# Score products of an attention group claimed early and joined into one run, on one core

## The chip, the cores and the metric

The kernel runs on one core of one Trainium2 chip. The metric is device time in microseconds (us) from the start to the end of one execution; lower is better. The matrix products run on TensorE, which the profile shows as PE (products) and PEld (loads of the stationary operand). VectorE is DVE, ScalarE is ACT, GpSimd is POOL and SyncE is SP. The banks in which products arrive (PSUM) are tiles of 128 rows of 512 float32 values in this kernel.

## The reference

The reference is a network of six layers over 256 positions of width 1024. Layers 0 to 3 each have a mixer, a norm and a feed-forward part; layers 0 and 3 mix by sliding-window attention, layer 1 by three dilated windows, layer 2 by attention within a block. Two further layers follow that have, among other branches, a differential attention. What the change touches is one thing in all of them, the scores of queries against keys:

```python
s = jnp.einsum('bnqhgd,bnkhd->bnhgqk', qb, kb) * (dh ** -0.5)     # layers 0 to 3, dh = 64
s = jnp.where(ok[None, :, None, None], s, NEG)
m = s.max(-1)
p = jnp.exp(s - m[..., None])
...
scores = jnp.einsum('bqhmd,bkhmd->bhmqk', qb, kh)                 # the two layers behind, 64 wide
p = jax.nn.softmax(jnp.where(mask, scores, -jnp.inf), axis=-1)
```

## The kernel before

The 256 positions are two blocks of 128 rows (t = 0 and 1). Each block is a stream of work of its own, written as a Python generator; `run` takes turns between the two and between small tasks that the streams spawn. That sets the order in which the program is written. A scheduler of the language then makes the final order on each engine: of what is ready by its own estimate of times, it takes what was written first (a priority can be raised for a stretch of code), and it hands out buffers. Each engine works its list strictly in that order.

Weights come by DMA as float32 (`raw`) and are split into a high and a low part by ScalarE (line 396) and VectorE (line 400). A projection is then three products per piece, lines 409 to 411, each 128 rows deep and 512 columns wide. These make up most of TensorE's time.

Attention works on groups of four heads. Queries and keys are transposed, so that the 64 values of a head lie on partitions: two heads (`par` = 0 and 1) share a tile, on partitions 0 to 63 and 64 to 127. `scores` (line 614) makes the group's products: for two tiles (`a`), t + 1 blocks of keys (`j`) and the two halves (`par`), so 4 products for t = 0 and 8 for t = 1. Each uses 64 rows of the array. The two halves write two different banks, `svs[0]` and `svs[1]`, tiles `ch` of a pool of three. There are 56 such groups. Then VectorE adds the mask to each bank (line 621, or 618 in the layers behind) and takes the maxima (line 636), ScalarE takes the exponentials (line 641, tile `pexp`), TensorE transposes these (line 664, tile `tp`), ScalarE copies them (line 666, tile `pt`), and TensorE multiplies by the values (line 652) into a third `ch` bank. Output transpositions (line 456, tile `ob`) and the output projection (tile `ho`) follow. The pool `ch` of three banks is shared by both streams, and by the sums of the feed-forward parts.

The order of a group's products among the others is not fixed in the code. The scheduler gives out the bank of `par` 0 and that of `par` 1 as each comes free, and puts other ready work between the products. Line 905 transposes a few parameters with 4 to 44 rows.

Of the kernel before, what the change touches and what calls it, by code (L numbers as in the profile page):

```python
# [11 lines left out]
BF16 = mybir.dt.bfloat16  # L12
# [6 lines left out]
P = 128  # L19
# [58 lines left out]
W_QK_2 = 3  # L78
W_BRANCH = 1
W_PARAMS = 6  # L80

DOWN = 1


class Net:
# [112 lines left out]
    def more_tables(self):  # L198
# [9 lines left out]
        for name, dil in (("b1", 4), ("b2", 16)):  # L208
# [5 lines left out]
                                    base=0, channel_multiplier=-1)  # L214
            yield from self.idle(W_PARAMS)
            pr = self.tpt()
# [387 lines left out]
    def scores(self, t, q, k, mask):  # L604

        nc = self.nc
        nk = (t + 1) * P
        svs = [self.bank().rearrange("p (h k) -> p h k", k=256)[:, :, :nk] for _ in range(2)]  # L610
        for a in range(2):
            for j in range(t + 1):
                for par in range(2):
                    nc.tensor.matmul(svs[par][:, a, j * P:(j + 1) * P], q(par, a), k(par, a, j), start=True, stop=True)  # L614
        for sv in svs:
            if mask is None:
                m = self.mask["b0"][:, None, P:].to_broadcast([P, 2, P])
                nc.vector.tensor_add(sv[:, :, t * P:], sv[:, :, t * P:], m)
            else:
                m = mask[:, None, (1 - t) * P:].to_broadcast([P, 2, nk])  # L620
                nc.vector.tensor_add(sv, sv, m)
        return svs
# [262 lines left out]
    def params_2(self, i):  # L885
# [4 lines left out]
        def cols(key, name, parts, scale=1.0):  # L890
# [3 lines left out]
            for src, k, rows in parts:  # L894
                self.small(raw[:rows, o:o + P * k], src)
                o += P * k
            yield from self.idle(W_PARAMS)
            n = sum(k * rows for _, k, rows in parts)
# [15 lines left out]
        def job():  # L914
# [4 lines left out]
            for k, name, n in (("kg", "da_k_norm_g_2", 64), ("qg", "da_q_norm_g_2", 64), ("sg", "da_subln_g_2", P),  # L919
                               ("dtb", "ssm_dt_bias_2", 16), ("al", "ssm_a_log_2", 16), ("d", "ssm_d_2", 16)):  # L920
                p[k] = self.row(self.bp.tile([P, n], F32, name=name, tag=name, bufs=1), io[name][i])
            yield from self.idle(W_PARAMS)
            tp = self.blocks_t(ws.rearrange("p g t -> p (g t)"), 4)
# [599 lines left out]
```

## Time and profile before

| | |
|---|---|
| time, median of 3 runs | 2391.38 us (2390.16 to 2392.42) |
| time of the profiled execution | 2393.47 us |
| its span, from the first to the last instruction | 2391.8 us |
| busy: PE, PEld | 2358.1 us (99%), 1922.7 us (80%) |
| busy: DVE, ACT, POOL | 1744.3 us (73%), 1314.9 us (55%), 124.7 us (5%) |
| mean granted TensorE clock | 0.997 of full speed |

Busy time is the time in which at least one instruction of an engine is under way. Products overlap in the pipeline: the start of one to the start of the next says more than the length of one. An idle time of PE is named with what ended it, in square brackets behind a row.

### The profile page before, as it was taken

To read this page: it belongs to the slowest core of one execution; us is meant where nothing else is said; L and a number is where in the kernel's file an instruction comes from. 1 tells how busy PE (TensorE), PEld (TensorE's weight loads), DVE (VectorE), ACT (ScalarE), POOL (GpSimd) and SP (SyncE) were. 2 spreads that over 40 slices of the span, in tenths; PEclk is the share of its full clock that TensorE was granted. 3 is DMA by queue.
4 is the path that set the end of the run, shared out by engine and by line. 5 is a ranking of instruction groups with operands and counts; after the bars stand their busy time and mean duration, and the time that the engine had idled before them with its cause. 6 is when DMAs were issued, how large, how long until landed. Compare 5 with 4: busy or idle time off the path is not lost.

```text
span 2391.8 us, 34975 instructions
## 1 busy us (share of the span) xinstructions
PE 2358.1 (99%) x11664; PEld 1922.7 (80%) x11664; DVE 1744.3 (73%) x4282; ACT 1314.9 (55%) x2180; POOL 124.7 (5%) x411
## 2 busy tenths in 40 slices
PE   8999999999999999999999999999999999999999
PEld 6888888888888788887788877877888778788887
DVE  7765676666755767557775588987877889987876
ACT  5454456655544555444544445744677657545776
POOL 1000000000000000000000000100011201000111
PEclk9999999999999999999999999999999999999999
DMA  6366554444566635665366567467566686575653
GB/s 234 100 207 187 176 176 131 135 128 128 182 188 187 192 124 173 191 187 184 112 193 191 186 134 168 127 150 203 161 191 186 170 186 128 123 216 171 187 184 115
DMA packets 280117, 400.16 MB, mean 167 GB/s; under 512 B 20588, under 2 KB 205098, under 8 KB 279936
## 3 DMA queue, kind: packets, MB, share of 16 engines
q1 hardware_dynamic: 274784, 381.88, 55.4%
q0 software_dynamic: 5152, 16.05, 2.2%
q8 instruction: 92, 1.51, 0.3%
q14 instruction: 89, 0.73, 0.1%
HBM read 396.81 MB, written 1.05 MB: 166 GB/s over the span
## 4 chain that ended last, share of the span: by engine, by line
PE 87%; DVE 7%; DMA 3%; ACT 2%; issue 1%; SPq 0%; ACTq 0%; DVEq 0%
PE pj L409 21%; PE pj L411 21%; PE pj L410 21%; PE tp L456 4%; PE ch L409 4%; PE ch L411 4%; PE ch L410 4%; PE ch L614 3%; PE ch L652 3%; DVE w L400 2%; DMA raw<-in_w_in_dram 2%; PE tp L664 1%; ACT w L396 1%; DVE convy L1003 1%; DMA raw<-in_w_branch_c_dram 0%
## 5 line engine op out<-in xcount | busy, mean ns | idle before, releaser
L400 DVE TENSOR_TENSOR w<-raw,w 128x512 fp32r<-128x512 f32 x1456 | 956.3, 683 | 456.6 <-ACT w L396 455.1
L396 ACT CAST w<-raw 128x1024 fp32r<-128x1024 f32 x728 | 759.0, 1043 | 661.5 <-PE pj L411 361.0
L409 PE MATMUL pj<-w,xth 128*128 128x512 f32 x2048 | 821.7, 402 | 4.3 <-ACT w L396 1.6
L410 PE MATMUL pj<-w,xth 128*128 128x512 f32 x2048 | 806.1, 394 | 2.9 <-DVE w L400 2.9
L411 PE MATMUL pj<-w,xtl 128*128 128x512 f32 x2048 | 805.1, 394 | 0.7 <-DVE xtl L448 0.7
L409 PEld LDWEIGHTS pj<-w,xth 128*128 128x128 f32 x2048 | 386.4, 189 | 89.3 <-ACT xth L447 5.7
L411 PEld LDWEIGHTS pj<-w,xtl 128*128 128x128 f32 x2048 | 386.3, 189 | 85.4 <-DVE xtl L448 3.0
L410 PEld LDWEIGHTS pj<-w,xth 128*128 128x128 f32 x2048 | 386.9, 189 | 80.6 <-DVE w L400 5.3
L409 PE MATMUL ch<-w,fht 128*128 128x512 f32 x412 | 171.9, 417 | 1.8 <-ACT fht L447 1.8
L411 PE MATMUL ch<-w,fht 128*128 128x512 f32 x412 | 161.9, 393 | 0.0
L410 PE MATMUL ch<-w,fht 128*128 128x512 f32 x412 | 161.2, 391 | 0.0
L1003 DVE SCALAR_TENSOR_TENSOR convy<-xc,ffn_cw,convy 128x128 f32<-128x128 f32 x352 | 100.5, 345 | 7.1 <-POOL ffn_hist L994 2.1
L411 PEld LDWEIGHTS ch<-w,fht 128*128 128x128 f32 x412 | 77.3, 188 | 18.4 <-DVE fht L448 1.0
L409 PEld LDWEIGHTS ch<-w,fht 128*128 128x128 f32 x412 | 77.4, 188 | 15.5 <-ACT fht L447 3.9
L410 PEld LDWEIGHTS ch<-w,fht 128*128 128x128 f32 x412 | 77.9, 189 | 12.2
L641 ACT ACTIVATE pexp<-ch,nm 128x128 f32<-128x128 f32 (+1 forms) x192 | 65.9, 421 | 36.8 <-DVE nm L636 24.0
L845 ACT ACTIVATE ffg<-pj 128x256 f32<-128x256 f32 x88 | 33.9, 386 | 76.1 <-PE pj L411 76.0
L1000 ACT ACTIVATE convy<-xc,ffn_cw 128x128 f32<-128x128 f32 x176 | 72.8, 484 | 1.4
L652 PEld LDWEIGHTS ch<-v,pt 128*128 128x128 f32 x576 | 70.6, 191 | 2.9
L409 PE MATMUL pj<-w,fht 128*128 128x512 f32 x180 | 71.3, 396 | 0.0
L411 PE MATMUL pj<-w,fht 128*128 128x512 f32 x180 | 70.7, 393 | 0.0
L410 PE MATMUL pj<-w,fht 128*128 128x512 f32 x180 | 70.1, 389 | 0.0
(338 smaller groups left out, 2706.2 us busy)
## 6 DMA issues: line engine op xcount, KB each, us to landing
raw<-in_w_gate_up_dram SPq DMA_DIRECT2D x352, 256.0 KB, 3.3
raw<-in_w_in_dram SPq DMA_DIRECT2D x128, 512.0 KB, 5.0
raw<-in_w_down_dram SPq DMA_DIRECT2D x88, 512.0 KB, 3.6
raw<-in_ffn_w_up_dram SPq DMA_DIRECT2D x176, 256.0 KB, 3.3
raw<-in_b_w_qkv_dram SPq DMA_DIRECT2D x144, 256.0 KB, 3.1
raw<-in_ffn_w_down_dram SPq DMA_DIRECT2D x44, 512.0 KB, 4.4
raw<-in_a_w_qkv_dram SPq DMA_DIRECT2D x24, 512.0 KB, 4.5
raw<-in_c_w_qkv_dram SPq DMA_DIRECT2D x48, 256.0 KB, 3.1
```

The costliest lines, as they stand in the source:

```text
L396: nc.scalar.copy(w[:, 0, :m], raw)
L400: self.last_low = nc.vector.tensor_sub(w[:, 1, s], raw[:, s], w[:, 0, s].bitcast(F32)).ins
L409: mm(ps, xh[:, k, :], wh[:, kk, cols], start=start, stop=False)
L410: mm(ps, xh[:, k, :], wl[:, kk, cols], start=False, stop=False)
L411: self.last_mm = mm(ps, xl[:, k, :], wh[:, kk, cols], start=False, stop=stop).ins
L456: self.nc.tensor.transpose(tp[:, b * P:(b + 1) * P], src[:, b * P:(b + 1) * P], self.ident)
L614: nc.tensor.matmul(svs[par][:, a, j * P:(j + 1) * P], q(par, a), k(par, a, j), start=True, stop=True)
L641: nc.scalar.activation(p[:, a, :(t + 1) * P], sv[:, a, :], AF.Exp, bias=n2[:, a:a + 1])
L652: nc.tensor.matmul(o[:, par + 2 * a, :], pts[par][:, a * (t + 1) + j, :], v(j, par + 2 * a), start=j == 0, stop=j == t)
L845: nc.scalar.activation(g, ps[:, :FFC], AF.Silu)
L1000: nc.scalar.activation(y[:, a, :], xc[:, a, 4:], AF.Identity, bias=b[:, 0, c:c + 1], scale=w[:, h, c:c + 1])
L1003: nc.vector.scalar_tensor_tensor(y[:, a, :], xc[:, a, o:o + P], w[:, j, c:c + 1], y[:, a, :], op0=OP.mult, op1=OP.add)
```

## The change

`scores` now opens each group with a claim, a product of one column by one (bfloat16, both operands the first column of the identity's bits) into the first value of the bank `svs[0]`, which the real products overwrite. The group's products may come only after the claim. The first of them (`par` 1, last block of keys) writes the other bank. All others come after that one, with their priority raised by 2000, which is far ahead in the order; and `par` and `j` are counted downwards.

```diff
+RUN = 2000
...
         svs = [self.bank().rearrange("p (h k) -> p h k", k=256)[:, :, :nk] for _ in range(2)]
-        for a in range(2):
-            for j in range(t + 1):
-                for par in range(2):
-                    nc.tensor.matmul(svs[par][:, a, j * P:(j + 1) * P], q(par, a), k(par, a, j), start=True, stop=True)
+        with ExitStack() as c:
+            o = self.ident.bitcast(BF16)[:, :1]
+            claim = nc.tensor.matmul(svs[0][:1, 0, :1], o, o, start=True, stop=True)
+            c.enter_context(self.tc.issue_after(claim.ins))
+            for a in range(2):
+                for j in range(t, -1, -1):
+                    for par in (1, 0):
+                        m = nc.tensor.matmul(svs[par][:, a, j * P:(j + 1) * P], q(par, a), k(par, a, j),
+                                             start=True, stop=True)
+                        if (a, j, par) == (0, t, 1):
+                            c.enter_context(self.tc.issue_after(m.ins))
+                            c.enter_context(self.tc.high_priority(RUN))
```

In the new program line 409 of before is line 411, 614 is 622, 652 is 664 and 664 is 676. The claims are line 617.

The first place is in layer 1, the order on TensorE around a group of the second block of rows. Before, its banks are `ch_3849` (`par` 0) and `ch_3850` (`par` 1):

```order
L411 MATMUL pj_3775<-w_3779,xtl_2872 128x512
L614 MATMUL ch_3849<-zt_3425,zt_3803 128x128
L614 MATMUL ch_3849<-zt_3632,zt_3803 128x128
L614 MATMUL ch_3849<-zt_3425,zt_3803 128x128
L614 MATMUL ch_3849<-zt_3632,zt_3803 128x128
L409 MATMUL pj_3805<-w_3597,xth_2998 128x512
L410 MATMUL pj_3805<-w_3597,xth_2998 128x512
L614 MATMUL ch_3850<-zt_3425,zt_3803 128x128
L614 MATMUL ch_3850<-zt_3632,zt_3803 128x128
L614 MATMUL ch_3850<-zt_3425,zt_3803 128x128
L614 MATMUL ch_3850<-zt_3632,zt_3803 128x128
L411 MATMUL pj_3805<-w_3597,xtl_2999 128x512
```

The four products of one bank stand together, two projection products come between, and then the four of the other bank. With the change the same group has the banks `ch_3863` and `ch_3864`:

```order
L617 LDWEIGHTS ident_88
L617 MATMUL ch_3863<-ident_88 1x1
L411 MATMUL pj_3818<-w_3609,xth_3006 128x512
L412 MATMUL pj_3818<-w_3609,xth_3006 128x512
L413 MATMUL pj_3818<-w_3609,xtl_3007 128x512
L411 MATMUL pj_3818<-w_3609,xth_3006 128x512
L622 MATMUL ch_3864<-zt_3644,zt_3816 128x128
L622 MATMUL ch_3863<-zt_3644,zt_3816 128x128
L622 MATMUL ch_3864<-zt_3436,zt_3816 128x128
L622 MATMUL ch_3863<-zt_3436,zt_3816 128x128
L622 MATMUL ch_3864<-zt_3644,zt_3816 128x128
L622 MATMUL ch_3863<-zt_3644,zt_3816 128x128
```

The claim stands four projection products ahead of the group, and all eight products (two more of the same kind follow) stand in one run that changes the bank with each. Over the whole program the 336 products stood in 74 runs, and stand in 56 now. Of the 56 claims 27 stand between two products that use the whole array; 29 stand directly before or behind a run of scores. Three claims stand some hundred products ahead of their group.

The second place is in layer 0, at the group of the second key head of the second block of rows. Before, its last score product is followed by 3 projection products, 4 transpositions and 12 projection products, and then by these rows (`pexp_760` and `pexp_765` are the exponentials of this group):

```order
L664 MATMUL tp_802<-ident_88,pexp_700 128x128 x2
L652 MATMUL ch_869<-v_262,pt_795 128x65
L664 MATMUL tp_807<-ident_88,pexp_705 128x128 x2
L652 MATMUL ch_869<-v_262,pt_795 128x65
L652 MATMUL ch_869<-v_262,pt_800 128x65
L664 MATMUL tp_824<-ident_88,pexp_737 128x128 x4
L664 MATMUL tp_831<-ident_88,pexp_742 128x128 x4
L652 MATMUL ch_869<-v_262,pt_800 128x65
L652 MATMUL ch_882<-v_262,pt_805 128x65
L664 MATMUL tp_838<-ident_88,pexp_760 128x128 x4
L664 MATMUL tp_845<-ident_88,pexp_765 128x128 x4
```

With the change its exponentials are `pexp_766` and `pexp_771`, and the end of the group and what follows stand so:

```order
L622 MATMUL ch_751<-zt_453,zt_652 128x128
L622 MATMUL ch_752<-zt_314,zt_652 128x128
L622 MATMUL ch_751<-zt_314,zt_652 128x128
L676 MATMUL tp_808<-ident_88,pexp_704 128x128 x2
L676 MATMUL tp_813<-ident_88,pexp_709 128x128 x2
L664 MATMUL ch_875<-v_262,pt_801 128x65
L676 MATMUL tp_830<-ident_88,pexp_742 128x128 x4
L676 MATMUL tp_837<-ident_88,pexp_747 128x128 x4
L676 MATMUL tp_844<-ident_88,pexp_766 128x128 x4
L664 MATMUL ch_875<-v_262,pt_801 128x65
L664 MATMUL ch_875<-v_262,pt_806 128x65
L676 MATMUL tp_851<-ident_88,pexp_771 128x128 x4
```

The projection products that stood between the group and the transpositions of its exponentials stand ahead of the group now. The same group of layer 3 has the same order.

## Rows read from the trace of the kernel before

**Rows 1.** The page: busy time by engine; the chain that ended last, by engine.
```profile
PE 2358.1 (99%) x11664; PEld 1922.7 (80%) x11664; DVE 1744.3 (73%) x4282; ACT 1314.9 (55%) x2180; POOL 124.7 (5%) x411
...
PE 87%; DVE 7%; DMA 3%; ACT 2%; issue 1%; SPq 0%; ACTq 0%; DVEq 0%
```

**Rows 2.** Groups of PE: line, count | busy us, mean ns | idle before.
```profile
L614 PE MATMUL ch<-zt 64*128 64x128 f32 x576 | 61.5, 291 | 0.0
...
L614 PE MATMUL ch<-dk,dq 64*128 64x128 f32 x96 | 8.1, 288 | 0.0
```

**Rows 3.** Timeline of PE, a run of eight alternating: start us, busy us.
```profile
320.57 0.40 PE L409 MATMUL pj<-w,xth 128*128 128x512 f32 x1
...
321.04 0.40 PE L411 MATMUL pj<-w,xtl 128*128 128x512 f32 x1
321.36 0.72 PE L614 MATMUL ch<-zt 64*128 64x128 f32 x8
...
322.34 0.40 PE L410 MATMUL pj<-w,xth 128*128 128x512 f32 x1
```

**Rows 4.** Timeline of PE, a run of sixteen alternating.
```profile
354.38 0.39 PE L411 MATMUL pj<-w,xtl 128*128 128x512 f32 x1
354.70 1.16 PE L614 MATMUL ch<-zt 64*128 64x128 f32 x16
...
356.13 0.39 PE L410 MATMUL pj<-w,xth 128*128 128x512 f32 x1
```

**Rows 5.** Timeline of PE, two runs of eight, each on one bank (`ch_3849`, `ch_3850`).
```profile
384.92 0.40 PE L411 MATMUL pj<-w,xtl 128*128 128x512 f32 x1
385.25 1.16 PE L614 MATMUL ch<-zt 64*128 64x128 f32 x8
...
386.67 0.40 PE L410 MATMUL pj<-w,xth 128*128 128x512 f32 x1
387.00 1.16 PE L614 MATMUL ch<-zt 64*128 64x128 f32 x8
```

**Rows 6.** Timeline of PE, one transposition of a tile of 4 rows.
```profile
1426.76 0.39 PE L411 MATMUL pj<-w,xtl 128*128 128x512 f32 x1
1427.08 0.22 PE L905 MATMUL tp<-ident,colsraw 4*128 4x4 f32 x1
1427.23 0.50 PE L409 MATMUL pj<-w,xth 128*128 128x512 f32 x1
1427.57 0.39 PE L410 MATMUL pj<-w,xth 128*128 128x512 f32 x1
```

**Rows 7.** Timeline of PE, transpositions of 44 rows mixed with score products.
```profile
1483.36 0.37 PE L614 MATMUL ch<-dk,dq 64*128 64x128 f32 x1
1483.46 0.24 PE L905 MATMUL tp<-ident,colsraw 44*128 44x44 f32 x1
```

**Rows 8.** Timeline of PE, layer 0, from the last scores to their transposed exponentials.
```profile
64.79 0.27 PE L614 MATMUL ch<-zt 64*128 64x128 f32 x1
...
65.42 1.16 PE L614 MATMUL ch<-zt 64*128 64x128 f32 x8
...
71.08 0.44 PE L664 MATMUL tp<-ident,pexp 128*128 128x128 f32 x2 [0.41 <-ACT pt L666]
...
73.48 1.14 PE L664 MATMUL tp<-ident,pexp 128*128 128x128 f32 x8
```

**Rows 9.** Timeline of PE, transpositions in a row.
```profile
91.78 0.82 PE L664 MATMUL tp<-ident,pexp 128*128 128x128 f32 x6
```

**Rows 10.** Timeline of DVE, masks and maxima of one group.
```profile
84.08 1.30 DVE L621 TENSOR_TENSOR ch<-ch,mask_a 128x512 f32<-128x512 f32 x2
85.28 1.28 DVE L636 TENSOR_REDUCE nm<-ch 128x2 f32<-128x512 f32 x2
```

**Rows 11.** Timeline of ACT, the exponentials of the same group.
```profile
86.74 1.57 ACT L641 ACTIVATE pexp<-ch,nm 128x256 f32<-128x256 f32 x4 [3.10 <-DVE nm L638]
```

**Rows 12.** Groups of DVE, the weight subtractions.
```profile
L400 DVE TENSOR_TENSOR w<-raw,w 128x512 fp32r<-128x512 f32 x1456 | 956.3, 683 | 456.6 <-ACT w L396 455.1
```

## The prediction

> **What bounds the kernel now.** I read the page first. TensorE is busy 99% of the span, VectorE 73%, ScalarE 55%, and the chain that ended last lies 87% on TensorE [rows 1]. The reader is to see that the order of the work, not a transfer, sets the time: a nanosecond less on TensorE is a nanosecond less in the end, as long as its next product is ready, and a product that isn't ready costs in full. Then the groups of TensorE by line. The score products of line 614 are 576 + 96 records (each of the 336 float32 products of the program is two) and keep the engine busy for 61.5 + 8.1 = 69.6 us, 2.9% of the span [rows 2]. They are the only work that the change touches on purpose.
>
> Last the timeline of TensorE around such products, where one record's start to the next tells what each costs. Two plain 512-wide products take 320.57 to 321.04 and so 0.23 us each. From the product ahead of a run of eight score records to the second product behind it are 321.04 to 322.34, 1.30 us, where two plain products would take 0.46: the run costs 0.84 us, of which 0.72 is its own busy time and 0.12 lies in the products around it [rows 3]. A run of sixteen costs 354.38 to 356.13 less 0.46, 1.29 us, for a busy time of 1.16 [rows 4]. These two runs alternate between the banks, and so between the upper and the lower 64 rows of the array. Where a run has only one bank, eight records already cost 384.92 to 386.67 less 0.46, 1.29 us, and the other half again 1.29 [rows 5]. So two records on different halves of the array go side by side; a pair costs about what one alone does; and a group that is torn into two one-bank runs costs 2.58 us instead of 1.29.
>
> **The change part by part.** *Joined groups.* In the order of before the 336 products stand in 74 runs, in that of the change in 56, one for each group: 28 of four products (eight records) and 28 of eight (sixteen), all alternating. By the rows for whole alternating runs their busy time becomes 28 x 0.72 + 28 x 1.16 = 52.6 us, 17.0 less than 69.6. Eighteen runs fewer also save what lies around a run, 18 x 0.12 = 2.2 us. Together -19.2 us. All of it is on the engine that sets the end, and the number of other products stays the same. The order in which a group's products stand (lower half first, last block first) changes nothing in this, since a pair still alternates.
>
> *Claims.* There are 56 new products of one column by one, each with its own weight load. They read the identity, which is there from the start, and in the order of the change only 4 of the 56 wait on another engine, so as waits they cost next to nothing; what would stand behind a waiting one are the projection products after it. But a claim uses 128 rows and one column of the array, another shape than the full products around it, and the trace has such a change: the transposition of a 4-row tile between full products. The product ahead of it takes 1426.76 to 1427.08, 0.32 instead of 0.23, it takes 0.15 itself, and the product behind it 0.34 instead of 0.23: 1427.57 - 1426.76 - 0.46 = 0.35 us in all [rows 6]. That is the upper bound for a claim between two full products. The transposition loads 128 columns of weights and the claim one; the first score record of a run shows what an exposed load of 128 columns is worth (0.37 us against 0.27 for those inside a run, as the row of the single record at 1483.36 and that at 64.79 have it [rows 7, 8]), 0.10, so the low end with a change of shape is 0.25. I take 0.30, the middle. 27 claims stand so: 8.1 us. The other 29 stand directly at a run of scores. There the array changes shape anyway, and only the claim's own time is added: 0.15 by the transposition's row, nothing at best. I take 0.05, since the rows where transpositions of 44 rows and score products stand mixed show a next start 0.10 us later and no gap of a change between the two shapes [rows 7]. 29 x 0.05 = 1.5. Together +9.6 us; with a change of shape between 27 x 0.25 = 6.8 and 27 x 0.35 + 29 x 0.15 = 13.8; if one narrow column needs no change of shape at all, between 0 and, at 0.05 for each, 2.8.
>
> The Trainium skill speaks against the claims: "TensorEngine Tiling (Array Packing)", section Tiling Modes, Key Properties, says that a change of tiling mode, not merely of the tile, drains the engine. The rows agree for full to row-tiled and back (0.09 and 0.11 us); the mixed rows at 1483 show two row tilings without that gap, so they bear the rule out only in part. By it the sum would be that of rival 2 below.
>
> *Waits.* A group now starts only when both banks are free, and both halves then go to VectorE at once. In layers 1 and 2 and in the second block nothing comes of it: after the joined group of the example 20 products of 0.23 us and 4 transpositions of 0.11 ((0.82 - 0.27) / 5 [rows 9]) still stand between the group and the transpositions of its exponentials, 5.0 us. What that has to cover is the softmax chain. For a group of 256 keys in layer 0 VectorE has the masks of both banks from 84.08 on, then the maxima, to 86.56, and ScalarE four exponentials from 86.74 to 88.31, so two in the first half of 1.57 [rows 10, 11]: the first bank's pair is there at 87.5, 3.4 us after the first mask began, the second's at 88.31, 4.2 us after. Both lie under 5.0. In layers 0 and 3, whose mixers have less other work, it is different. There the group of the second key head of the second block of rows is followed, in the order of the change, by twelve transpositions and one small product (two records, 0.11 each like the transpositions) before its own exponentials are wanted, 12 x 0.11 + 0.22 = 1.5 us; in before 66.58 to 73.48, 6.9 us, lay between [rows 8]. TensorE would wait 3.4 - 1.5 = 1.9 us for the first bank and some 0.3 more for the second. In layer 0 the head before it has six products, that group, four transpositions and the small product as cover, 1.4 + 1.3 + 0.4 + 0.2 = 3.3 us, and stands on VectorE just ahead, for which I add 1.0. That is 2.2 + 2.2 + 1.0 = 5.4 us, less the 0.41 that before waits at this place [rows 8]: +5.0. What is late then is everything behind it on TensorE: the output products, the output projection and the norm of that block of rows. Bounds: 0, if the products behind are ready and the scheduler's estimate is right, and 4 x 3.4 = 14 if two heads in each of the two layers wait a whole chain.
>
> Sum: -19.2 + 9.6 + 5.0 = -4.6 us. The profiled execution took 2393.47 us for a span of 2391.8 and lies 2.1 above the median of 2391.38; applied to the median the sum gives 2386.8, **2387 us**.
>
> **Rivals.**
> 1. *The claim is free.* If one column goes through without a change of shape, the claims cost 2.8 and the sum is -19.2 + 2.8 + 5.0 = -11.4: 2380 us. For it: no row shows a tile of weights with all rows and few columns, so nothing says that it pays. Against it: every row with another shape than the full one pays at either side.
> 2. *Every change of shape pays, the one between a claim and a run too.* Then the 29 claims at a run cost what the transposition does less the exposed load of the product behind, which the run pays anyway: 0.25, and the others 0.35: 7.3 + 9.5 = 16.7, sum +2.5: 2394 us. For it: the two gaps of rows 6. Against it: rows 7. This is what that rule of the Trainium skill would make of it.
> 3. *The softmax chain becomes the wait, and the kernel is slower.* Each of the 28 groups of 256 keys now gives VectorE two masks and two maxima in one piece. If two weight subtractions of 0.68 us [rows 12] come between them, the chain is 4.2 + 1.4 = 5.6 us, and the 5.0 us of cover (with the 0.2 of the run's exit 5.2) leave 0.4 in each: 11 us more, sum +6.6: 2398 us. It decides from 0.34 us a group on, where it takes the gain and 4.8 us besides. For it: VectorE is 73% busy and half of that is these subtractions. Against it: the chain at 84 us shows 4.2, and the masks are wanted at the same rate as before.
> 4. *The gain is hidden.* TensorE runs ahead and waits for weights instead, and the time stays at 2391. Against it: weights are made by ScalarE and VectorE, which both have idle time [rows 1].
>
> **How the numbers follow.** The likeliest case has a chance of 0.50 and its own range is 2382 to 2392, by the claims' 6.8 to 13.8 and by the waits. Rival 1 has 0.25, rival 2 0.12, rival 3 0.08, rival 4 0.05. What this kernel's measurement can tell from no change is about 0.2%, 4.8 us, and so a time below 2386.6 counts as faster: a little under half of the likeliest case and nearly all of rival 1, 0.24 + 0.25 = 0.49. Slower, over 2396.2, are rival 3 and a tail of rival 2, 0.11. The rest is 0.40. For 8 in 10 the range runs from 2378, within rival 1, to 2394, the middle of rival 2.
>
> **What would show it.** The busy time of the score products should fall from 69.6 to about 52.6 us, in 56 runs of 0.72 and 1.16. A claim between full products should show 0.32 us ahead of it and about 0.33 behind; if these are 0.23, rival 1 holds; if a claim that stands directly ahead of a run adds 0.2 or more, rival 2 does. TensorE should wait about 2 us for the exponentials (line 653 of the kernel after) in the mixers of layers 0 and 3 and nowhere else. Waits for them in layer 1 mean rival 3. The prediction is wrong if the claim's price lies outside 0 to 0.35 us, or if waits appear that the two orders don't suggest, such as for a bank that a claim holds early.

## The result and the profile after

The change makes the kernel slower: 2404.94 us (median of 4 runs, 2401.92 to 2408.31) against 2391.74 us for the kernel before on the same chip, a ratio of 1.0056 (95% interval 1.0039 to 1.0074), or 13 us more. Five later runs of the change give 2403.07 us and 1.0049 (1.0036 to 1.0063). The prediction was 2387. The profiled execution after took 2402.53 us.

Page of the kernel after: busy time by engine, and the chain that ended last by engine [rows 1].

```profile
PE 2353.1 (98%) x11720; PEld 1917.9 (80%) x11720; DVE 1743.7 (73%) x4282; ACT 1313.1 (55%) x2180; POOL 122.8 (5%) x411
...
PE 86%; DVE 7%; DMA 4%; ACT 2%; issue 1%; ACTq 0%; DVEq 0%; SPq 0%
```

TensorE is busy 5.0 us less than before, and yet the span is 9.0 us longer (2400.8 against 2391.8). So it stands idle 14.0 us more. The view of instruction groups has the products the change is about; line 617 is the claim [rows 2].

```profile
L622 PE MATMUL ch<-zt 64*128 64x128 f32 x576 | 45.1, 289 | 3.7 <-ACT pexp L653 3.7
L676 PE MATMUL tp<-ident,pexp 128*128 128x128 f32 x288 | 43.4, 290 | 9.5 <-ACT pt L678 9.5
L617 PE MATMUL ch<-ident 128*1 128x1 bf16 x56 | 9.2, 164 | 0.0
L622 PE MATMUL ch<-dk,dq 64*128 64x128 f32 x96 | 7.5, 289 | 0.0
```

The scores take 45.1 + 7.5 = 52.6 us, as forecast. New are the idle times at the right: 3.7 us ahead of scores and 9.5 us ahead of the transpositions of the exponentials. The windows say where TensorE stands still (columns: stretch, its length, busy time of PE, granted clock, DMA). First the kernel after, then the one before, for layer 0, layer 3 and a stretch of the last layer:

```profile
0.00:104.00 104.00, 87.57 (x511) 0.97 0.52 170
...
1150.00:1210.00 60.00, 53.10 (x359) 0.94 0.26 80
...
2040.00:2110.00 70.00, 65.52 (x319) 0.93 0.56 123
```

```profile
0.00:104.00 104.00, 92.81 (x516) 1.00 0.52 170
...
1150.00:1210.00 60.00, 58.94 (x368) 1.00 0.27 83
...
2040.00:2110.00 70.00, 68.26 (x343) 0.98 0.60 143
```

Idle time rises by 16.43 - 11.19 = 5.2 us in layer 0, by 6.90 - 1.06 = 5.8 us in layer 3 and by 4.48 - 1.74 = 2.7 us behind 2040; that is 13.7 of the 14.0. In the same three stretches the granted clock is lower. The timeline of TensorE in layer 0 of the kernel after:

```profile
69.17 1.16 PE L622 MATMUL ch<-zt 64*128 64x128 f32 x16 [2.54 <-ACT pexp L653]
75.08 1.12 PE L676 MATMUL tp<-ident,pexp 128*128 128x128 f32 x4 [4.75 <-ACT pt L678]
...
76.32 2.58 PE L676 MATMUL tp<-ident,pexp 128*128 128x128 f32 x12
```

The second group of 256 keys (sixteen records) waits 2.54 us, and the first transposition behind it 4.75 us. Layer 3 has the same two waits, 1.20 and 4.76 us. Before, 0.41 us was waited at this place [rows 8]. What each wait is for stands in ScalarE's timeline of the same stretch:

```profile
68.28 1.57 ACT L653 ACTIVATE pexp<-ch,nm 128x256 f32<-128x256 f32 x4 [4.04 <-DVE nm L650]
...
73.20 1.57 ACT L653 ACTIVATE pexp<-ch,nm 128x256 f32<-128x256 f32 x4 [3.27 <-DVE nm L650]
74.64 0.66 ACT L678 COPY pt<-tp 128x256 f32<-128x256 f32 x2
```

The group starts at 69.17, when the first two exponentials of the group before it are done (half of 1.57 us from 68.28 on): these free its second bank. There are three `ch` banks; the claim has one, the group before has the other two. The transpositions at 75.08 need a `tp` bank, of which there are two. Both still hold transposed exponentials, which ScalarE copies out only at 74.64, because the copies stand in its list behind the four exponentials of the last group. These need the scores of 69.17 and VectorE's masks and maxima. So TensorE waits for the whole chain of the group that it has just issued, at a point ahead of all the work that I had counted as cover.

The granted clock in the same two places, kernel after (all 1.00 in the kernel before):

```profile
70.00:74.00 4.00, 0.33 (x6) 0.70 0.00 0
74.00:78.00 4.00, 2.92 (x14) 0.50 0.00 0
78.00:82.00 4.00, 4.00 (x37) 0.95 0.02 4
1174.00:1178.00 4.00, 1.78 (x9) 0.51 0.29 97
1178.00:1182.00 4.00, 4.00 (x26) 0.64 0.00 0
```

A window's clock gives the share of it at each of the two levels: 0.70 of 4 us is 2.4 us at half. If the half clock is one stretch in each place, TensorE has it from 71.6 to 78.4 and from 1174.1 to 1180.9, at the lower level, 1.2 instead of 2.4 GHz, and this outlasts the wait: it has work again from 75.08 and 1176.22. By estimate, half the speed in the 3.3 and 4.7 us left costs 1.7 + 2.3 = 4.0 us. The twelve transposition records take 2.58 us, where 12 x 0.11 = 1.3 would do.

To see where time is lost across the program I took the start of the same projection product (line 411 of before, 413 of after) in two traces. The difference, in us, against the trace before, for the change, its second profile, and experiments that follow:

```
start before | change  again | no claim  not 0,3  claim only  no claim, not 0,3  first four
        32.0 |  -0.30   0.15 |    -0.22     0.01       -0.26              -0.32       -0.75
        61.9 |  -3.04  -2.50 |     0.29    -0.17        0.58              -0.42       -3.17
       103.8 |   3.93   5.29 |     1.88    -0.17        1.06              -0.40        3.72
      1131.5 |   2.02   2.57 |     0.09    -2.50        3.46              -2.38        1.12
      1204.9 |   4.57   5.37 |     3.11    -2.48        4.39              -2.28        3.92
      2042.4 |   3.27   4.15 |     0.65    -4.08        4.04              -5.49        6.54
      2100.1 |   9.07   9.69 |     1.87    -1.22        4.74              -5.72        6.20
      2375.5 |   9.08   9.68 |     1.38    -1.72        4.73              -5.72        6.20
```

The change gains 2.7 us up to 61.9, loses 7.0 us in the rest of layer 0, gains 1.9 in layers 1 and 2, loses 2.6 in layer 3 and 5.8 between 2042 and 2100. The profiled run of before lies some 2 us above its median, so every column stands that much too low against medians.

### The profile page after: what moved, and what is told of

It reads as the page before. It is cut to its first block, busy times and chain, and to the rows that moved or that the text cites. A ratio compares the mean times of both kernels' runs of the same rounds, so it can differ in the third digit from the quotient of the medians.

```text
span 2400.8 us, 35060 instructions
## 1 busy us (share of the span) xinstructions
PE 2353.1 (98%) x11720; PEld 1917.9 (80%) x11720; DVE 1743.7 (73%) x4282; ACT 1313.1 (55%) x2180; POOL 122.8 (5%) x411
## 4 chain that ended last, share of the span: by engine, by line
PE 86%; DVE 7%; DMA 4%; ACT 2%; issue 1%; ACTq 0%; DVEq 0%; SPq 0%
PE pj L411 21%; PE pj L413 21%; PE pj L412 21%; PE tp L458 4%; PE ch L411 4%; PE ch L413 4%; PE ch L412 4%; PE ch L664 3%; DMA raw<-in_w_in_dram 2%; DVE w L402 2%; PE ch L622 2%; PE tp L676 2%; ACT w L398 1%; DMA raw<-in_a_w_qkv_dram 1%; DVE convy L1015 0%
```

## The experiments

All were timed in five rounds beside the kernel before. Each edit is against the kernel after unless another is named.

**No claim.**

```diff
-            claim = nc.tensor.matmul(svs[0][:1, 0, :1], o, o, start=True, stop=True)
-            c.enter_context(self.tc.issue_after(claim.ins))
```

> The group's products follow its first one with the raised priority as in the change, but nothing claims the bank ahead of them. In the order, 64 runs instead of 56 (74 before), and in the mixers of layers 0 and 3 four projection products and the old transpositions stand between the last group of 256 keys and the transpositions of its exponentials. Theory (the claim, not the joining, brings the order in which TensorE waits for the softmax chain): the 10.7 us of the claims and the waits and half clock of layers 0 and 3 are gone, and 10 of the 18 joined runs are left of the gain, -19.2 x 10/18 = -10.7: about 2381 us, ratio 0.9955. Rival (joining brings the waits): the claims' 10.7 go and the rest stays, 2394 us, ratio 1.001.

Measured 2398.75 us, ratio 1.0032 (1.0022 to 1.0043): between the two, and the theory is refuted as I put it. The wait of the scores is gone, but that of the transpositions remains, as the waits of TensorE show (us in total, times, longest):

```profile
PE tp L673 <- ACT pt L675: 6.4, 2, 3.7
```

So the claim makes the wait for the bank, and the joining by itself makes most of the other. In its order four projection products stand between the last bank and the transpositions in layer 0, and none in layer 3; before, it was twelve and eleven. That cover is too short: the theory had to look at the last bank of the group, not at its first product.

**Not in layers 0 and 3.** The second kernel is the mirror: its condition is `mask is not None and mask is self.mask["a"]`.

```diff
+        if mask is None or mask is not self.mask["a"]:
             with ExitStack() as c:
...
+        else:
+            for a in range(2):
+                for j in range(t + 1):
+                    for par in range(2):
+                        nc.tensor.matmul(svs[par][:, a, j * P:(j + 1) * P], q(par, a), k(par, a, j), start=True, stop=True)
```

> The change in layers 1 and 2 and in the two layers behind; layers 0 and 3 keep the old lines and their old order. Theory (the loss is made in the mixers of layers 0 and 3): layers 1, 2 and 4 give -2.4 + 0.5 - 1.1 = -3.0 us as between the two traces, 2389 us, ratio 0.9988, if the further 5.8 us lost at 2047 to 2106 us also go; 2394.5, ratio 1.001, if those belong to the later layers' own change. Rival (each claim costs its share wherever it stands): 40 of 56 claims, 13 x 40/56 = +9, 2401 us, ratio 1.004.

Measured 2391.67 us, ratio 1.0004 (0.9995 to 1.0012): no loss, no gain. None of the two waits is left.

> The mirror: the change in layers 0 and 3 alone, 16 claims, 61 runs. Theory: +3.9 in layer 0 and +2.6 in layer 3 as between the two traces, with the waits of 2.5, 4.8, 1.2 and 4.8 us and two stretches of half clock: 2398 us, ratio 1.003; 2404, ratio 1.005, if the loss at 2047 to 2106 us follows from these layers too. Rival (each claim costs its share): 13 x 16/56 = +3.7, 2395 us, ratio 1.0015, and no waits.

Measured 2400.37 us, ratio 1.0041 (1.0028 to 1.0054), with the waits of 9.5 and 3.7 us again. The two together put 9 of the 13 us on layers 0 and 3 (2400.37 against 2390.97), and refute a price that each claim pays wherever it stands. The two parts, 0.7 and 9.4 us, make 10.1 and not 12 or 13; the last layers, below, lose more when both are in.

**A claim of the array's full shape.**

```diff
-            claim = nc.tensor.matmul(svs[0][:1, 0, :1], o, o, start=True, stop=True)
+            claim = nc.tensor.matmul(svs[0][:, 0, :1], self.ident.bitcast(BF16)[:, :P], o, start=True, stop=True)
```

> The claim loads the whole identity (128 columns) and writes 128 x 1 values; the order is that of the change, row for row. It prices the change of shape. Theory (the claim between full products costs 0.295 us because of its shape, and 0.09 where the shape doesn't change): 27 x 0.2 = 5.4 us less than the change, 2399.5 us, ratio 1.003. Rival (the price is that of any product of one column): as the change, 2405, ratio 1.0055.

Measured 2397.69 us, ratio 1.0029 (1.0017 to 1.0041): 5.4 less than the change in the later measurement, 7.2 less than in the first. The same claim in layer 1, first in the kernel after:

```profile
338.81 0.40 PE L413 MATMUL pj<-w,xtl 128*128 128x512 f32 x1
339.14 0.16 PE L617 MATMUL ch<-ident 128*1 128x1 bf16 x1
339.23 0.72 PE L622 MATMUL ch<-zt 64*128 64x128 f32 x8
```

and with the full shape:

```profile
339.05 0.40 PE L413 MATMUL pj<-w,xtl 128*128 128x512 f32 x1
339.29 0.18 PE L617 MATMUL ch<-ident 128*128 128x1 bf16 x1
339.40 0.71 PE L622 MATMUL ch<-zt 64*128 64x128 f32 x8
```

The product ahead of the claim takes 0.24 us again instead of 0.33, so the narrow shape is what makes that product longer. From the claim to the run it is 0.09 against 0.11.

**The change again.**

> The change itself once more, for its spread and for a second profile. Theory (the waits of layers 0 and 3 are in the order and return with every run; the 5.8 us at 2047 to 2106 us, behind the last group of scores, are a matter of how that stretch happens to fall): waits of 3.7 us for the exponentials and 9.5 us for the transposed ones in both layers again, 2405 us, and another loss than 5.8 us at 2047 to 2106. Rival (that loss is made by the order of the change): 5 to 6 us there again.

Measured 2403.07 us. The waits of 9.5 and 3.7 us return, and 5.5 us are lost again between 2042 and 2100: here the rival holds. The clock varies. In this profile it falls in layer 0 already behind the first wait, and the score group runs at half speed (2.08 us instead of 1.16):

```profile
69.70 2.08 PE L622 MATMUL ch<-zt 64*128 64x128 f32 x16 [2.54 <-ACT pexp L653]
76.54 1.12 PE L676 MATMUL tp<-ident,pexp 128*128 128x128 f32 x4 [4.76 <-ACT pt L678]
```

**The claim alone.**

```diff
+        o = self.ident.bitcast(BF16)[:, :1]
+        claim = nc.tensor.matmul(svs[0][:1, 0, :1], o, o, start=True, stop=True)
+        with self.tc.issue_after(claim.ins):
             for a in range(2):
                 for j in range(t + 1):
                     for par in range(2):
                         nc.tensor.matmul(svs[par][:, a, j * P:(j + 1) * P], q(par, a), k(par, a, j), start=True, stop=True)
```

(against the kernel before)

> The claims ahead of the groups, with the products in the old order and without priority: 56 claims, 11 of them between full products, 80 runs instead of 74. Theory (layers 0 and 3 lose by the joining, the claims cost what their records show): no wait for the exponentials or the transposed ones in layers 0 and 3; 11 x 0.295 + 45 x 0.09 = 7.3 us for the claims and 6 runs more at 19.2/18 = 1.07 each, 6.4: 2404.5 us, ratio 1.0057. Rival (the claim itself brings the waits of layers 0 and 3): those waits are there, 11 us more, 2416 us.

Measured 2398.22 us, ratio 1.0034 (1.0022 to 1.0047). No wait appears in layers 0 and 3, which refutes the rival. It is 7.3 us more than before and not 13.7: the six more runs cost less than I expected, since the scores are busy for 63.1 + 8.2 = 71.3 us, 1.7 more than before, not 6.4. With 7.3 for the claims that is 9.0.

```profile
L621 PE MATMUL ch<-zt 64*128 64x128 f32 x576 | 63.1, 291 | 0.0
L621 PE MATMUL ch<-dk,dq 64*128 64x128 f32 x96 | 8.2, 289 | 0.0
```

**Joined without claims, not in layers 0 and 3.** The two edits above together.

> The joining without claims in layers 1, 2 and the layers behind, the old lines in layers 0 and 3: 69 runs, as many as with the claims there. Theory: the kernel with the claims in the same layers took 2391.7 us; its 40 claims (14 between full products) cost 14 x 0.295 + 26 x 0.094 = 6.6 us and bought nothing: 2385 us, ratio 0.9977. Rival (claims next to a run cost nothing that shows): 14 x 0.295 = 4.1 us, 2387.5, ratio 0.9987; rival (joining brings nothing): 2391, ratio 1.

Measured 2388.73 us, ratio 0.9992 (0.9983 to 1.0000): the best of all versions, but its interval reaches to no change. It is 3 us below the kernel with claims in the same layers, not 6.6, and by the table the 3 us are made behind 1204.9, where the two part by 4.2. In layers 1 and 2 they are alike, so the claims there do buy something. The 384 score records of layers 1 and 2, here without claims and then in the kernel with them:

```profile
L620 PE MATMUL ch<-zt 64*128 64x128 f32 x384 | 34.8, 289 | 0.0
```

```profile
L623 PE MATMUL ch<-zt 64*128 64x128 f32 x384 | 30.0, 289 | 0.0
```

Both have 69 runs, and I had counted runs. But a run can be whole and still not alternate between the banks; by busy time the claims save 4.8 us there, and by their records 32 of them (9 between full products) cost 9 x 0.295 + 23 x 0.094 = 4.8.

**TensorE kept busy in the wait.**

```diff
+        if t == 1 and mask is not None and mask is self.mask["a"]:
+            self.nth = getattr(self, "nth", -1) + 1
+            if self.nth % 4 == 1:
+                with self.tc.issue_after(m.ins), self.tc.high_priority(RUN):
+                    d = self.bank("pj")
+                    for n in range(18):
+                        nc.tensor.matmul(d[:, :P], self.ident, self.ident, start=True, stop=True)
```

> The change, and behind the second group of 256 keys in layers 0 and 3 eighteen products of the identity with itself (128 x 128, float32, some 0.22 us each, 4.0 us together), whose result nothing uses; they stand where TensorE waits 4.8 us. Theory (part of the loss is the half clock granted after the wait): the idle time shrinks to about 1 us, no stretch of half clock follows in these two layers, and about half of the 2.1 and 4.7 us that TensorE was busy at half clock behind the waits comes back: 3.4 us less than the change, 2401.5 us beside 2405. Rival (the half clock comes from elsewhere, or costs nothing): the time stays at 2405; or, if the products delay what follows, 2409.

Measured 2396.85 us, ratio 1.0022 (1.0011 to 1.0032): 6 to 8 us less than the change, with 36 products more. Layer 3 of this kernel:

```profile
1169.45 1.16 PE L622 MATMUL ch<-zt 64*128 64x128 f32 x16 [1.20 <-ACT pexp L660]
1170.54 4.29 PE L633 MATMUL pj<-ident 128*128 128x128 f32 x36
1175.37 0.44 PE L683 MATMUL tp<-ident,pexp 128*128 128x128 f32 x2 [0.55 <-ACT pt L685]
```

```profile
70.00:74.00 4.00, 4.00 (x30) 0.60 0.09 26
74.00:78.00 4.00, 4.00 (x36) 0.97 0.00 0
1170.00:1174.00 4.00, 4.00 (x43) 1.00 0.77 232
1174.00:1178.00 4.00, 3.46 (x31) 1.00 0.11 35
```

The real work starts at the same distance from the group as in the change (5.92 us), but the clock stays at 1.00, and the stretch from 1131.5 to 1204.9 loses 0.5 us instead of 2.6. In layer 0 the clock falls nevertheless, behind the wait of 2.55 us for the bank that stands ahead of the filling, and little is won: 6.4 us are lost behind 61.9 instead of 7.0. So half speed is a part of the loss, and the 2.1 us that layer 3 gets back lie near the 2.3 estimated for it. The products behind the filling also stand in another order, so not all of it need be the clock. The rest of the gain, 4 to 6 us by the medians, isn't explained by the filling: of the 4.9 us between the two profiled spans (2400.8 and 2395.9), 1.4 are made between 2042 and 2100, where no filling stands.

**The last two layers alone, and the first four.** The old lines stand in the branch not taken.

```diff
+        if self.passed >= 3:
```

```diff
+        if self.passed < 3:
```

> The change in the two layers behind alone (8 groups, 8 claims, 5 of them between full products); layers 0 to 3 keep the old lines and order. Theory (the loss at 2047 to 2106 us is made by the groups of the last layers, whose claims and places change the order of TensorE behind them): 3 to 6 us are lost in that stretch, 2395 us, ratio 1.0017. Rival (it is the timing that the earlier layers leave, not the order): no loss there, 2391 us, ratio 1.

Measured 2393.84 us, ratio 1.0009 (1.0000 to 1.0018); 2.0 us are lost between 2042 and 2100.

> The change in layers 0 to 3 alone (48 claims); the two layers behind keep the old lines, and TensorE's order there is that of before to the end. Theory: the 5.5 to 5.8 us at 2047 to 2106 us are not lost, all else is as with the change: 2404 - 5.6 = 2398.5 us, ratio 1.003. Rival (they come from the timing that the earlier layers leave): 2404 us, ratio 1.0055.

Measured 2399.68 us, ratio 1.0039 (1.0026 to 1.0051); nothing is lost in that stretch (6.54 to 6.20). So the loss there comes with the last layers' own groups, whose place moves some projection products and transpositions in the order behind them, and not with the state in which the earlier layers leave the engines alone. The waits of TensorE in this stretch, in the kernel after, sum to 4.4 us, against 1.1 + 0.5 before. The two largest:

```profile
PE ch L1131 <- DVE ssl L1127: 2.3, 2, 1.6
PE ch L1120 <- ACT state L1110: 1.4, 1, 1.4
```

Its size does depend on more: 2.0 us with the change in these layers alone, 2.9 with layers 1 and 2, 5.5 and 5.8 with all. TensorE's idle time is not what differs: 4.3 of the 70 us in the kernel without the change in layers 0 and 3, 4.5 in the kernel after. The granted clock is. First that kernel, then the one with the full-shaped claim; the kernel after has 0.93 in this stretch:

```profile
2040.00:2110.00 70.00, 65.68 (x330) 0.98 0.61 143
2040.00:2110.00 70.00, 66.28 (x328) 0.95 0.59 137
```

Read as above, 0.98, 0.95 and 0.93 are about 3, 7 and 10 of the 70 us at half clock. Where the last layers have the change, the loss goes with that: 2.0 and 2.9 us at 0.98, 3.4 with the full-shaped claim and 4.4 with the filling at 0.95, 5.5 and 5.8 at 0.93, so about half a microsecond for each one more at half clock. Some 2 to 3 us are thus the order's own, and the rest goes with the clock; why it stays low for longer in some kernels, is open. Joined without claims, the last layers lose little there: nothing with the old lines in layers 0 and 3 (-5.49 to -5.72 in the table), 1.2 us where all layers are joined (0.65 to 1.87). The kernel with the change in layers 0 to 3 alone also loses 2.6 us between 1204.9 and 2042.4 in its profile, where TensorE has half its clock for 6.8 us from 1644.7 on; no other profile has that.

**The copies on VectorE.**

```diff
-        nc.scalar.copy(pt[:, :m, :], tp[:, :m * P].rearrange("p (b t) -> p b t", t=P))
+        (nc.vector.tensor_copy if dve else nc.scalar.copy)(pt[:, :m, :], tp[:, :m * P].rearrange("p (b t) -> p b t", t=P))
```

(`dve` is set in layers 0 and 3)

> The change, with the copies of the transposed exponentials on VectorE instead of ScalarE in layers 0 and 3. On ScalarE they stand behind the exponentials of the last group, which end at 74.7 us; on VectorE they stand behind its maxima, which end at 73.3. Theory (TensorE's 4.8 us wait ends when these copies run, and what holds them is the engine's list behind the last group): the wait for them is some 1.4 us shorter in each layer, 2.8 us less than the change and up to 2 more if the half clock behind it gets shorter: 2400 us, ratio 1.004. Rival (the copies wait for something else, or TensorE then waits for the exponentials of the group itself instead): 2404, ratio 1.0055.

Measured 2402.12 us (2396.96 to 2409.16), ratio 1.0057 (1.0043 to 1.0071). As a time that is inconclusive. The wait itself does what the theory says: 3.37 us in layer 0, 1.38 less than 4.75, and it ends with VectorE's copy. In both layers together this wait is 6.7 us instead of 9.5, but the scores wait 4.7 instead of 3.7, so 1.8 of the expected 2.8 us are left; and TensorE has half its clock for some 10 us in layer 3, where it was 6.8 with the change.

```profile
69.20 1.16 PE L622 MATMUL ch<-zt 64*128 64x128 f32 x16 [2.79 <-ACT pexp L653]
73.73 1.11 PE L676 MATMUL tp<-ident,pexp 128*128 128x128 f32 x4 [3.37 <-DVE pt L678]
```

**Joined without claims, but for the groups of 256 keys in layers 0 and 3.**

```diff
+        self.g0 = mask is not None and mask is self.mask["a"]
...
+        if not ((self.g0 and t == 1)):
```

(against the kernel without claims)

> The joining without claims everywhere but in the groups of 256 keys of layers 0 and 3 (8 groups, old lines); 66 runs. Against the kernel that joins everywhere without claims (2398.75 us), the last bank of the second such group in each of layers 0 and 3 comes 12 and 11 projection products ahead of the transpositions of the group before, where it came 4 and none ahead. Theory (what costs the time is that the last group of 256 keys has no projection products left behind it): no waits for the copies of the transposed exponentials, no half clock in these layers, some 10 us less: 2388 us, ratio 0.9985. Rival (what costs is the joining as such in layers 0 and 3, the groups of 128 keys too): half of it stays, 2394 us, ratio 1.0015.

Measured 2391.10 us, ratio 1.0000 (0.9991 to 1.0009). Eight groups less, and 7.6 of the 7.8 us that joining without claims lost are back. None of TensorE's time around these groups is at half clock. It is not 2388: waits of 2.4 us for the copies remain.

```profile
PE tp L682 <- ACT pt L684: 2.4, 2, 1.4
```

## Why the prediction was wrong

**Joined groups: right.** 56 runs, and 52.6 us of busy time, to the tenth. The 2.2 us for the edges of eighteen runs were not measured by themselves. By place, layers 0 and 3 give 25.5 - 15.0 = 10.5 us of it, layers 1 and 2 36.0 - 30.0 = 6.0, the last layers 8.1 - 7.5 = 0.6 (old and new sums in the kernels with the change in one part only; 61.5 - 25.5 = 36.0).

**Claims: right in size.** Forecast +9.6 us. A claim between full products shows 0.33 us ahead, 0.09 itself and 0.34 behind, 0.295 more than two plain products; a claim at a run adds 0.094 where I took 0.05: 27 x 0.295 + 29 x 0.094 = 10.7. One of the 27, in layer 3 of the kernel after:

```profile
1155.25 0.40 PE L413 MATMUL pj<-w,xtl 128*128 128x512 f32 x1
1155.58 0.17 PE L617 MATMUL ch<-ident 128*1 128x1 bf16 x1
1155.67 0.50 PE L411 MATMUL pj<-w,xth 128*128 128x512 f32 x1
1156.01 0.39 PE L412 MATMUL pj<-w,xth 128*128 128x512 f32 x1
```

That 0.30 was so close is in part luck: its low end, 0.25, took off 0.10 us for a load of 128 columns, and the full-shaped claim, which loads as many, costs less than the narrow one (0.13 us against 0.30), not more. Rival 1, a free claim, falls with the price of 0.30, and the full-shaped claim shows why. Rival 2 falls too, as none at a run adds 0.2. The rule of the Trainium skill on which rival 2 stood, "TensorEngine Tiling (Array Packing)", section Tiling Modes, Key Properties, that a change of mode drains the engine, agrees with the trace ahead of and behind full products (0.33 and 0.34 us instead of 0.23), and not for the step from a narrow claim to a run (0.09 us).

**Waits: the step that failed.** It gave +5.0 us, with bounds of 0 to 14; measured are 5.2 + 5.8 = 11.0 us of idle time in layers 0 and 3, and, by the estimate above, 4.0 more at half clock: 15.0. The place was right, the mechanism only in part. The bounds, too, were dropped on the way: with 0 to 14 for the waits and 6.8 to 13.8 for the claims the sum goes from 2379 to 2400 us, and the range of the likeliest case, 2382 to 2392, gave no reason for leaving most of that out. I let TensorE go on through "twelve transpositions and one small product" and wait for the group's own exponentials behind them. In fact it stops at the first of the twelve, because a `tp` bank has to come free, and the copy that frees it stands in ScalarE's list behind those same exponentials:

```
L653 ACTIVATE pexp_766<-ch_751,nm_750 128x256 x2
L653 ACTIVATE pexp_771<-ch_752,nm_750 128x256 x2
L678 COPY pt_801<-tp_798 128x256
L678 COPY pt_806<-tp_803 128x256
```

The same copies stood behind the same exponentials before (kernel before, layer 0):

```profile
68.47 2.29 ACT L641 ACTIVATE pexp<-ch,nm 128x256 f32<-128x256 f32 x6
70.62 0.68 ACT L666 COPY pt<-tp 128x256 f32<-128x256 f32 x2
```

What changed is that the projection products, twelve of them directly ahead of that point in layer 0 and eleven in layer 3, no longer stood on TensorE between the last scores and these transpositions. I had read TensorE's order alone. The second thing I missed is the wait for a bank that the claim makes (2.54 and 1.20 us). The text named it as what would make the prediction wrong, "a bank that a claim holds early", and gave it no price; it had asked only whether the claims themselves wait. The third is the clock, which no term had. The Trainium skill speaks of it: "TensorE: Matmul & The Clock Gate", section "Why this matters for your kernels", advises against pauses between bursts of products, since the clock then drops to half. The trace agrees: 0.50 and 0.51 in the windows in which the waits of 4.75 and 4.76 us end.

**What no term had.** "In layers 1 and 2 and in the second block nothing comes of it" holds for layers 1 and 2, but the last two layers lose 5.8 us between 2042 and 2100: by the runs above some 2 to 3 us with the order of their own groups, the rest with the lower clock.

The sum with what was measured: -19.2 + 10.7 + 15.0 + 5.8 = +12.3 us. The spans differ by 9.0, or 10.1 without 1.1 us that the profile of before lost by itself at 1381 to 1455; the medians differ by 13.2 and, in the second measurement, 12.2. Rival 3 (slower, softmax chain exposed) had the sign and the chain, but in the groups of layer 1, where no wait appeared. Rival 4 falls, as TensorE does not wait for weights more than before.

## What to carry to other kernels

Joining products into dense runs moves the filling between them to another place, and what it covered there has to be looked up: for each wait the question is which buffer comes free when, and what stands ahead of the freeing instruction on its own engine's list, not only what stands behind the products on TensorE. A price per place is better than a sum: the same edit gained 1.9 us in layers 1 and 2 and, by itself, cost 9 us in layers 0 and 3. And a count of runs was a poor measure of how well products pack; their busy time is the better one.

## What the runs showed of the hardware

A wait on TensorE can cost twice, since the lower clock outlasts it: 6.8 us at 1.2 GHz around each wait of 4.8 us, by estimate 4.0 us of work lost to it in the two layers. With one such wait filled by products that nothing uses, in layer 3, the clock stayed at 1.00. The lower clock came behind shorter pauses too, and not behind each: the same wait of 2.54 us in layer 0 was followed by full speed in the first profile of the change (1.16 us for the group) and by half in the second (2.08). In the kernel with the change in layers 0 and 3 alone, a wait of 1.70 us for a weight in a stretch that is busy 2.30 of 4 us is followed by a clock of 0.57 while TensorE is fully busy:

```profile
833.60 0.41 PE L458 MATMUL tp<-ident,stg 128*128 128x128 f32 x2 [1.70 <-ACT w L398]
```

```profile
830.00:834.00 4.00, 2.30 (x13) 1.00 0.90 303
834.00:838.00 4.00, 4.00 (x17) 0.57 0.41 138
```

A product of one column costs 0.30 us between full products as a 1 x 1 product, and 0.13 if it loads all 128 columns (0.24 ahead, 0.04 itself and 0.31 behind, less two plain ones).
